# Feed-forward: projecting parts 1 to 8 down in twos, with twelve products to a PSUM bank

## The chip, the cores and the metric

The kernel runs on one core of a Trainium2 chip. The metric is the time of the whole kernel on the device in microseconds; lower is better. A core has five engines that work side by side, each through its own queue in order: TensorE (PE) multiplies matrices into PSUM, VectorE (DVE), ScalarE (ACT) and GpSimd (POOL) work on elements, and SyncE (SP) issues the transfers (DMA) from and to memory.

## The reference, cut to what matters

The program is a two-layer encoder over two sequences, 512 tokens ("sample") and 256 ("prompt"), 768 columns in all, with 1024 channels. Each layer has a mixer and then a feed-forward block, in float32. The change lies in the feed-forward:

```python
def conv_ffn(h, w_up, conv_w, conv_b, w_down):
    u = h @ w_up                      # 1024 -> 2 * 2816 channels
    u = conv(u, conv_w) + conv_b      # width 3 along the tokens, each channel alone
    g = u[..., :D_FF]
    val = u[..., D_FF:]
    return (jax.nn.silu(g) * val) @ w_down   # 2816 -> 1024

x = x + g2 * conv_ffn(h, ...)         # g2: a gate for each channel and sequence
```

## The kernel before, in words

Activations lie transposed in SBUF, channels on the 128 partitions and tokens along the row. Every product of two float32 matrices is made of three products of a high and a low part: weight high by activation high, weight high by activation low, weight low by activation high. The high part is a cast by ScalarE, the low part a subtraction by VectorE (`fp_copy_split`, lines 271 to 279).

The feed-forward of a layer (`ffn`, line 1582 on) cuts the 2816 hidden channels into eleven parts of 256 (`NPART` = 11). A part has three units of weights, each loaded by SP in two halves of 512 KB into one of five `raw` buffers and split into one of three `whi` and three `wlo` buffers (`split`, lines 290 to 293).

`up(p)` makes the hidden values of a part. Two calls of `pair` (gate channels, then value channels) multiply by a scheme of seven quarter products instead of eight; each quarter is twelve products of 384 columns (lines 1360 to 1363). A pair holds three split weight tiles at once (`wa`, `wc`, `wb`); `wc` and `wb` need sums of weight quarters that GpSimd makes from `raw` (lines 1393 to 1405), and between quarters ScalarE copies one bank into another, the fork copies (lines 1409 and 1420). The first part's ups, and a piece of the second's, are made in `head`. After each pair the convolution runs on two rows of channels: one ScalarE instruction and two of VectorE for each row (lines 1597, 1599 and 1600). Then `silu` on ScalarE (1607), and `product`: GpSimd multiplies (1612), and the result is split into its high and low part in a tile `g`.

`down(p, g)` multiplies `g` by the part's third unit: for each of its two weight halves four output tiles of 512 columns and four of 256, six products to a PSUM bank, then one VectorE instruction (the eviction, `resid`, line 604) that multiplies the bank by the gate and adds it to the residual stream `xt`. So a part has 96 down products and 16 evictions. The banks come from `pa`, four of them. The last part works in three ranges of 256 columns and starts the next norm.

The order of the program is up 0, up 1, down 0, up 2, down 1, and so on to up 10, down 9, down 10. Each engine's queue is then ordered by a planner that goes through the program with modelled costs: an instruction that stands later in the program may come earlier on its engine where the earlier one is not ready. So in the trace down products lie among the quarter products of the next part. A call within `issue_after` puts what it holds behind a named instruction on that engine. `held` is a list of work that is put off: `pair` takes one entry and issues it behind its fork copy (line 1420).

Long rows lie in six `slab` buffers. During the ups two hold `xt`, one the rows `urow`, and the rest `yrow` (the convolved rows of a part) and `g`. The tiles `urow` of the first part are a slab of their own, free after its convolution.

Of the kernel before, what the change touches and what calls it, by code (L numbers as in the profile page):

```python
# [12 lines left out]
R = mybir.dt.float32r  # L13
# [3 lines left out]
P = 128  # L17
# [7 lines left out]
RANGES = ((256, 512, 0), (512, 768, 0), PROMPT)  # L25
# [5 lines left out]
TG = T + GAP  # L31
# [3 lines left out]
NPART = FC // 2  # L35
# [45 lines left out]
def col(t):  # L81

    return t + (GAP if t >= 256 else 0)
# [7 lines left out]
class Norm:  # L91
# [31 lines left out]
    held = False  # L123
# [58 lines left out]
class Net:  # L182
# [1399 lines left out]
    def ffn(self, l, xt, pool, last_tile, apply, keep=None):  # L1582
        nc = self.nc
        u0 = U_FFN + l * NPART * 3
        early = self.prepare(u0)
        next(last_tile)

        urows = [self.slab([P, 4, TG]) for _ in range(2)]
        for urow in urows:
            nc.gpsimd.memset(urow[:, :, 256 : 256 + GAP], 0.0)  # L1590

        behind = []

        def conv(u, y, ch):
            cb = self.cst(CB + l * 44 + ch)
            w = lambda tap: self.cst(CW + (l * 44 + ch) * 3 + tap)
            nc.scalar.activation(y, u, AF.Identity, bias=cb, scale=w(1))  # L1597
            stt = nc.vector.scalar_tensor_tensor
            stt(y[:, 1:], u[:, :-1], w(0), y[:, 1:], ALU.mult, ALU.add)  # L1599
            stt(y[:, :-1], u[:, 1:], w(2), y[:, :-1], ALU.mult, ALU.add)  # L1600


        held = []

        def silu(yrow):
            for j in range(2):
                nc.scalar.activation(yrow[:, j], yrow[:, j], AF.Silu)

        def product(yrow, g):
            for j in range(2):  # L1610
                y = yrow[:, 2 + j]
                nc.gpsimd.tensor_tensor(y, y, yrow[:, j], ALU.mult)  # L1612
                self.fp_copy_split(g[:, 0, j], g[:, 1, j], y)

        def up(p):
            urow = urows[0] if p == 0 else urows[1]
            fixed = lambda i: self.bank[i][:, :H]
            if p == 0:
                eng = mybir.EngineType
                self.ready(HALVES[0])  # L1620
                with self.tc.manual_schedule(engines={eng.PE, eng.Activation, eng.DVE}):
                    behind[:] = self.head(u0, last_tile, pool, urows, mark, early)
            yrow = self.slab([P, 4, TG])
            g = self.slab([P, 2, 2, TG], R)
            for i in range(2):
                if p:
                    rows = [urow[:, 2 * i + j] for j in range(2)]
                    with ExitStack() as order:
                        for ins in behind[2 * i :] if p == 1 else ():
                            order.enter_context(self.tc.issue_after(ins))  # L1630

                        other = p == i == 1
                        bank = lambda j: self.pa()[:, :H] if j == 1 and other else fixed(j)
                        self.pair(pool, u0 + 3 * p + i, bank, rows, p == 1, held.pop() if held else None)
                for j in range(2):
                    conv(urow[:, 2 * i + j], yrow[:, 2 * i + j], i * FC + 2 * p + j)
                if i == 0:
                    held.append(lambda: silu(yrow))
            if p:
                product(yrow, g)  # L1640
            else:
                gate = held.pop()
                held.append(lambda: (gate(), product(yrow, g)))
            return g

        def mark(t):

            hi, _ = self.quarter(self.B11)
            self.mm(t, hi[0][:, :P], hi[0], True, True)

        def down(p, g):
            ws = (w for _, w in self.halves(u0 + 3 * p + 2))
            chunk = lambda w, i: [t[:, 512 * i : 512 * (i + 1)] for t in w]

            def tile(w, c, rng, more=False):
                s0, s1, _ = rng
                alone = keep is None and p == NPART - 1
                o = (self.ps() if more and (c % 2 or alone) else self.pa())[:, : s1 - s0]
                cs = slice(c % 4 * P, (c % 4 + 1) * P)
                for i in range(2):  # L1660
                    wh, wl = chunk(w, i)
                    gh, gl = (g[:, z, i, col(s0) : col(s0) + s1 - s0] for z in range(2))
                    self.mm(o, wh[:, cs], gh, i == 0, False)
                    self.mm(o, wh[:, cs], gl, False, False)
                    self.mm(o, wl[:, cs], gh, False, i == 1)
                return self.resid(xt, o, l, 40, c, rng)

            if p < NPART - 1:
                for h, w in enumerate(ws):
                    for rng in SAMPLE, PROMPT:  # L1670
                        for c in range(4 * h, 4 * h + 4):
                            tile(w, c, rng, p == NPART - 2)
                return
            ws = list(ws)
            for rng in RANGES:
                final = keep is None and rng is RANGES[-1]
                norm = Norm(
                    self, xt, rng, apply, 3 if final else 4 if keep is None and rng is RANGES[1] else 2, final,
                    wait=0.0 if keep is None or rng is RANGES[-1] else 1.3,
                )  # L1680
                for c in range(KC):
                    done = tile(ws[c // 4], c, rng, keep is None or rng is not RANGES[-1])
                    norm.square(c)
                    if final and c >= KC - 2:
                        self.ends.append(done.ins)
                    if final and c == KC - 1:
                        norm.sums = [norm.sums[i] for i in (1, 2, 0, 3)]
                        norm.begin(1)
                    self.tick(0.65)
                if keep is not None:  # L1690
                    self.save_x(xt, keep, rng)
                self.start(rng, norm.stages())

        prev = None
        for p in range(NPART):
            g = up(p)
            if prev is not None:
                down(*prev)
            prev = (p, g)
        down(*prev)  # L1700


    def run(self):
# [179 lines left out]
```

## Time and profile before

| | |
|---|---|
| time, median of 3 runs | 1803.56 us (1803.45 to 1805.8) |
| the profiled execution | 1807.31 us, of which its span is 1805.3 us |
| VectorE, share of the span | 77% |
| ScalarE | 50% |
| GpSimd | 28% |
| evictions and gated sums of line 604, 128x512 from `pa` | 152, 743 ns each |
| of 128x256 from `pa` | 168, 476 ns each |

The profile is of one execution. Busy time of PE is modelled from the starts of its products, which overlap, so the distance between starts says more than the length of one. Rows of a timeline give the start, the length, the engine, the line of the kernel, the operation, the tiles written and read, the shape and the count of instructions merged into the row; a bracket at the end gives the engine's idle time before it and who ended that.

### The profile page before, as it was taken

The page shows a single profiled execution, that of the slowest core. Times are in us where ns is not written, and L with a number is a line of the kernel's source. Part 1 is how long each engine was busy: PE and PEld are TensorE (multiplying, and loading weights), DVE is VectorE, ACT ScalarE, POOL GpSimd, SP SyncE. Part 2 cuts the span into 40 slices and gives each one's busy share as a digit, 9 for nine tenths or more (in the row PEclk, how much of TensorE's full clock was granted, in tenths as well). Part 3 has the DMA queues.
Part 4 walks back from the last instruction along what each step waited for, and adds up shares of the span by engine and source line. Part 5 has one row for each costly group of instructions (what it writes and reads, how often), then busy time and mean ns, then how long its engine had stood idle before and what let it go on. Part 6 is the DMA issues. An engine that isn't in the chain of part 4 may idle for free.

```text
span 1805.3 us, 28807 instructions
## 1 busy us (share of the span) xinstructions
PE 1765.0 (98%) x11140; PEld 1641.3 (91%) x11140; DVE 1397.3 (77%) x2196; ACT 900.3 (50%) x1822; POOL 510.1 (28%) x433
## 2 busy tenths in 40 slices
PE   7999999989999999999999999999999999999998
PEld 4988888979998999999999999989989999999997
DVE  4876677996799777788877867767998777777877
ACT  4545443443564444444444657665564444444443
POOL 3001010231134233333331313320234333333323
PEclk9999999999999999999999999999999999999999
DMA  9354665467212222222222321234122222222212
GB/s 359 99 163 148 207 197 188 151 187 233 71 59 71 71 62 68 70 70 71 70 70 84 108 91 42 62 99 128 47 82 70 71 71 70 71 71 71 70 36 71
DMA packets 64996, 185.07 MB, mean 103 GB/s; under 512 B 6247, under 2 KB 24839, under 8 KB 64732
## 3 DMA queue, kind: packets, MB, share of 16 engines
q1 hardware_dynamic: 64284, 182.72, 31.8%
q8 instruction: 87, 1.43, 0.3%
q10 hardware_dynamic: 576, 0.52, 0.1%
q14 instruction: 49, 0.40, 0.1%
HBM read 176.77 MB, written 6.44 MB: 101 GB/s over the span
## 4 chain that ended last, share of the span: by engine, by line
PE 84%; DVE 6%; DMA 5%; ACT 3%; issue 2%; POOL 1%; SPq 0%; DVEq 0%; ACTq 0%; POOLq 0%
PE ps L269 26%; PE pa L269 23%; PE ps L1360 10%; PE ps L1361 10%; PE ps L1363 10%; DMA raw<-in_adaln_t_dram 2%; DVE junk L540 1%; PE pa L1199 1%; DMA raw<-in_w_dram 1%; DMA slab<-in_adaln_w_dram 1%; DVE wlo L276 1%; ACT whi L275 0%; PE pa L1360 0%; PE pa L1361 0%; PE pa L1363 0%
## 5 line engine op out<-in xcount | busy, mean ns | idle before, releaser
L275 ACT CAST whi<-raw 128x1024 fp32r<-128x1024 f32 (+1 forms) x231 | 241.0, 1045 | 339.2 <-PE pa L269 144.0
L276 DVE TENSOR_TENSOR wlo<-raw,whi 128x1024 fp32r<-128x1024 f32 (+1 forms) x231 | 318.5, 1380 | 112.7 <-ACT whi L275 110.0
L269 PE MATMUL pa<-slab,whi 128*128 128x256 f32 (+1 forms) x1280 | 307.6, 335 | 0.0
L269 PEld LDWEIGHTS pa<-slab,whi 128*128 128x128 f32 x1280 | 222.2, 188 | 21.6 <-DVE slab L604 0.4
L604 DVE SCALAR_TENSOR_TENSOR slab<-pa,mod,slab 128x256 f32<-128x256 f32 (+1 forms) x320 | 187.2, 603 | 61.4 <-PE pa L269 61.3
L269 PE MATMUL pa<-slab,wlo 128*128 128x512 f32 (+1 forms) x640 | 205.8, 334 | 0.0
L269 PE MATMUL ps<-zh,whi 128*128 128x256 f32 (+1 forms) x560 | 187.4, 336 | 5.0 <-ACT whi L275 4.8
L269 PE MATMUL ps<-zl,whi 128*128 128x256 f32 (+1 forms) x560 | 183.2, 330 | 0.5 <-DVE zl L565 0.5
L269 PE MATMUL ps<-zh,wlo 128*128 128x256 f32 (+1 forms) x560 | 180.6, 329 | 0.2 <-DVE wlo L276 0.2
L1360 PE MATMUL ps<-zh,whi 128*128 128x384 f32 x504 | 172.6, 343 | 3.8 <-ACT nt L1431 2.0
L269 PE MATMUL ps<-slab,whi 128*128 128x384 f32 (+2 forms) x704 | 172.0, 329 | 0.9 <-DVE slab L276 0.5
L1361 PE MATMUL ps<-zl,whi 128*128 128x384 f32 x504 | 170.0, 337 | 1.8 <-DVE zl L1317 1.8
L540 DVE CUSTOM_DVE_ANT_0 junk<-raw,crow,cstt 128x1024 f32<-128x1024 f32 x112 | 148.6, 1327 | 27.8 <-DMA raw<-in_adaln_t_dram 27.1
L1363 PE MATMUL ps<-zh,wlo 128*128 128x384 f32 x504 | 169.2, 336 | 0.0
L1396 POOL TENSOR_TENSOR raw<-raw,raw 128x512 f32<-128x512 f32 x40 | 53.7, 1342 | 318.5 <-DVE wlo L276 245.8
L1612 POOL TENSOR_TENSOR slab<-slab 128x772 f32<-128x772 f32 x44 | 86.4, 1966 | 168.8 <-DVE slab L1600 155.9
L269 PEld LDWEIGHTS pa<-slab,wlo 128*128 128x128 f32 x640 | 120.4, 188 | 13.2 <-DVE wlo L276 0.4
L1599 DVE SCALAR_TENSOR_TENSOR slab<-slab,cstt,slab 128x771 f32<-128x771 f32 x88 | 107.6, 1224 | 27.1 <-ACT slab L1597 26.9
L269 PEld LDWEIGHTS ps<-slab,whi 128*128 128x128 f32 x704 | 122.4, 188 | 3.4 <-ACT whi L275 0.9
L269 PEld LDWEIGHTS ps<-zh,whi 128*128 128x128 f32 x560 | 106.4, 190 | 18.2 <-ACT whi L275 5.0
L269 PE MATMUL ps<-slab,wlo 128*128 128x384 f32 (+2 forms) x352 | 114.8, 328 | 0.1
L269 PEld LDWEIGHTS ps<-zl,whi 128*128 128x128 f32 x560 | 106.3, 190 | 9.3 <-DVE zl L565 0.7
(304 smaller groups left out, 4297.2 us busy)
## 6 DMA issues: line engine op xcount, KB each, us to landing
raw<-in_w_dram SPq DMA_DIRECT2D x208, 512.0 KB, 3.8
raw<-in_adaln_t_dram SPq DMA_DIRECT2D x56, 512.0 KB, 4.1
raw<-in_adaln_w_dram SPq DMA_DIRECT2D x28, 512.0 KB, 4.4
slab<-in_x_dram SPq DMA_DIRECT2D x12, 512.0 KB, 8.2
slab<-in_adaln_w_dram SPq DMA_DIRECT2D x11, 512.0 KB, 9.2
slab<-mrows SPq DMA_DIRECT2D x8, 384.0 KB, 6.7
xs<-slab SPq DMA_DIRECT2D x6, 512.0 KB, 2.9
bt<-brow SPq DMA_DIRECT2D x16, 192.0 KB, 3.1
```

The lines of the kernel that those rows point to most:

```text
L269: self.nc.tensor.matmul(out, lhsT, rhs, start=start, stop=stop)
L275: nc.scalar.copy(hi, src)
L276: return nc.vector.tensor_tensor(lo, src, hi.bitcast(F32), ALU.subtract)
L540: nc.vector.tensor_tensor_reduce(out=junk, in0=w, in1=row[:, s], scale=1.0, scalar=self.cst(AB + 48 * l + j), op0=ALU.mult, op1=ALU.add, a ...
L604: return self.nc.vector.scalar_tensor_tensor(x, o, self.mod[l][:, gc + c, q : q + 1], x, ALU.mult, ALU.add)
L1199: nc.tensor.transpose(pp[:, ks], b.t[:, e, ks], self.ident)
L1360: mm(o, wh[:, k], hi[k], start=start and k == 0, stop=False, skip_group_check=True)
L1361: mm(o, wh[:, k], lo[k], start=False, stop=False, skip_group_check=True)
L1363: mm(o, wl[:, k], hi[k], start=False, stop=k == 3, skip_group_check=True)
L1396: tt(q[0], q[2], q[0], ALU.subtract)
L1599: stt(y[:, 1:], u[:, :-1], w(0), y[:, 1:], ALU.mult, ALU.add)
L1612: nc.gpsimd.tensor_tensor(y, y, yrow[:, j], ALU.mult)
```

## The change

Parts 1 to 8 go down in twos: after up 3 the parts 1 and 2, after up 5 the parts 3 and 4, after up 7 the parts 5 and 6, after up 9 the parts 7 and 8. Part 0 (after up 1), part 9 and part 10 (both after up 10) go alone as before. In a joined down both parts' products of one output tile go into one bank, twelve instead of six, and are evicted once. Both parts' weight halves are split and held together, first halves, then second halves.

The tile `g` is now made when it is first written, and `yrow` after the part's first pair. For the odd parts 3, 5, 7 and 9 GpSimd's multiplication stays where it was, and the split of its result is put into `held`, so that it comes behind the fork copy in the next part's first pair. The count of products, their columns and the loads are the same.

```diff
+        gs = {}
+
+        def product(yrow, p, now):
+            def part(j):
+                if not j:
+                    gs[p] = self.slab([P, 2, 2, TG], R)
+                self.fp_copy_split(gs[p][:, 0, j], gs[p][:, 1, j], yrow[:, 2 + j])
+
             for j in range(2):
                 y = yrow[:, 2 + j]
                 nc.gpsimd.tensor_tensor(y, y, yrow[:, j], ALU.mult)
-                self.fp_copy_split(g[:, 0, j], g[:, 1, j], y)
+                if now:
+                    part(j)
+            if not now:
+                held.append(lambda: [part(j) for j in range(2)])
...
             if p:
-                product(yrow, g)
+                product(yrow, p, p in (1, NPART - 1) or p % 2 == 0)
...
-        def down(p, g):
-            ws = (w for _, w in self.halves(u0 + 3 * p + 2))
+        def down(parts):
+            of = [self.halves(u0 + 3 * p + 2) for p in parts]
+            g = [gs.pop(p) for p in parts]
...
+                steps = [(w, x, i) for w, x in zip(ws, g) for i in range(2)]
+                for w, x, i in steps:
                     wh, wl = chunk(w, i)
-                    gh, gl = (g[:, z, i, col(s0) : col(s0) + s1 - s0] for z in range(2))
-                    self.mm(o, wh[:, cs], gh, i == 0, False)
+                    gh, gl = (x[:, z, i, col(s0) : col(s0) + s1 - s0] for z in range(2))
+                    self.mm(o, wh[:, cs], gh, w is ws[0] and i == 0, False)
                     self.mm(o, wh[:, cs], gl, False, False)
-                    self.mm(o, wl[:, cs], gh, False, i == 1)
+                    self.mm(o, wl[:, cs], gh, False, w is ws[-1] and i == 1)
                 return self.resid(xt, o, l, 40, c, rng)
...
-            if p < NPART - 1:
-                for h, w in enumerate(ws):
+            if parts[0] < NPART - 1:
+                for h in range(2):
+                    ws = [next(x)[1] for x in of]
                     for rng in SAMPLE, PROMPT:
                         for c in range(4 * h, 4 * h + 4):
-                            tile(w, c, rng, p == NPART - 2)
+                            tile(ws, c, rng, parts[-1] == NPART - 2)
                 return
...
-        prev = None
         for p in range(NPART):
-            g = up(p)
-            if prev is not None:
-                down(*prev)
-            prev = (p, g)
-        down(*prev)
+            up(p)
+            if p % 2:
+                down((p - 2, p - 1) if p > 1 else (0,))
+        down((p - 1,))
+        down((p,))
```

More of the change, by code (lines that the diff above doesn't have):

```diff
@@ L1607, in silu @@
                 nc.scalar.activation(yrow[:, j], yrow[:, j], AF.Silu)
-        def product(yrow, g):
+        gs = {}
[4 more added lines that the diff above has]
+                self.fp_copy_split(gs[p][:, 0, j], gs[p][:, 1, j], yrow[:, 2 + j])
             for j in range(2):
@@ L1622, in up @@
                     behind[:] = self.head(u0, last_tile, pool, urows, mark, early)
-            yrow = self.slab([P, 4, TG])
-            g = self.slab([P, 2, 2, TG], R)
+            yrow = None
             for i in range(2):
@@ L1634, in up @@
                         self.pair(pool, u0 + 3 * p + i, bank, rows, p == 1, held.pop() if held else None)
+                yrow = yrow or self.slab([P, 4, TG])
                 for j in range(2):
@@ L1639, in up @@
             if p:
-                product(yrow, g)
+                product(yrow, p, p in (1, NPART - 1) or p % 2 == 0)
             else:
                 gate = held.pop()
-                held.append(lambda: (gate(), product(yrow, g)))
-            return g
+                held.append(lambda: (gate(), product(yrow, p, True)))
         def mark(t):
@@ L1649, in mark, with tile @@
             self.mm(t, hi[0][:, :P], hi[0], True, True)
-        def down(p, g):
-            ws = (w for _, w in self.halves(u0 + 3 * p + 2))
+        def down(parts):
+            of = [self.halves(u0 + 3 * p + 2) for p in parts]
+            g = [gs.pop(p) for p in parts]
             chunk = lambda w, i: [t[:, 512 * i : 512 * (i + 1)] for t in w]
-            def tile(w, c, rng, more=False):
+            def tile(ws, c, rng, more=False):
                 s0, s1, _ = rng
-                alone = keep is None and p == NPART - 1
+                alone = keep is None and parts[0] == NPART - 1
                 o = (self.ps() if more and (c % 2 or alone) else self.pa())[:, : s1 - s0]
                 cs = slice(c % 4 * P, (c % 4 + 1) * P)
-                for i in range(2):
+                steps = [(w, x, i) for w, x in zip(ws, g) for i in range(2)]
+                for w, x, i in steps:
                     wh, wl = chunk(w, i)
-                    gh, gl = (g[:, z, i, col(s0) : col(s0) + s1 - s0] for z in range(2))
-                    self.mm(o, wh[:, cs], gh, i == 0, False)
+                    gh, gl = (x[:, z, i, col(s0) : col(s0) + s1 - s0] for z in range(2))
+                    self.mm(o, wh[:, cs], gh, w is ws[0] and i == 0, False)
                     self.mm(o, wh[:, cs], gl, False, False)
-                    self.mm(o, wl[:, cs], gh, False, i == 1)
+                    self.mm(o, wl[:, cs], gh, False, w is ws[-1] and i == 1)
                 return self.resid(xt, o, l, 40, c, rng)
-            if p < NPART - 1:
-                for h, w in enumerate(ws):
+            if parts[0] < NPART - 1:
+                for h in range(2):
+                    ws = [next(x)[1] for x in of]
                     for rng in SAMPLE, PROMPT:
                         for c in range(4 * h, 4 * h + 4):
-                            tile(w, c, rng, p == NPART - 2)
+                            tile(ws, c, rng, parts[-1] == NPART - 2)
                 return
-            ws = list(ws)
+            ws = [w for _, w in of[0]]
             for rng in RANGES:
@@ L1681, in down @@
                 for c in range(KC):
-                    done = tile(ws[c // 4], c, rng, keep is None or rng is not RANGES[-1])
+                    done = tile(ws[c // 4 : c // 4 + 1], c, rng, keep is None or rng is not RANGES[-1])
                     norm.square(c)
```

## The prediction

> **What bounds the kernel now.** I read the head of the page first.
>
> ```profile
> span 1805.3 us, 28807 instructions
> PE 1765.0 (98%) x11140; PEld 1641.3 (91%) x11140; DVE 1397.3 (77%) x2196; ACT 900.3 (50%) x1822; POOL 510.1 (28%) x433
> ```
>
> TensorE is busy nearly always, but a mean over stages proves nothing for the feed-forward, so I read a window over one of its parts, from the last product of one part's ups to that of the next. The columns are length, then busy time and instructions of PE, PE's weight loads, VectorE (DVE), ScalarE (ACT) and GpSimd (POOL), the granted clock, and the DMA engines' share and GB/s.
>
> ```profile
> 740.02:786.40 46.38, 46.38 (x266) 43.98 (x265) 37.49 (x42) 21.61 (x35) 16.69 (x10) 1.00 0.22 69
> ```
>
> One part is 46.4 us, all of it PE, at a granted clock of 1.00; DVE is busy 37 us of it. Since a busy PE could hide slow starts, the timeline must give the pace. These rows are a quarter product's first product and the next quarter's first, twelve on; then down products of 512 columns, two to a row; then of 256 columns, two and one.
>
> ```profile
> 773.59 0.34 PE L1360 MATMUL ps<-zh,whi 128*128 128x384 f32 x1
> ...
> 775.68 0.34 PE L1360 MATMUL ps<-zh,s1h 128*128 128x384 f32 x1
> ...
> 744.98 0.62 PE L269 MATMUL pa<-slab,whi 128*128 128x512 f32 x2
> 745.44 0.62 PE L269 MATMUL pa<-slab,wlo 128*128 128x512 f32 x2
> ...
> 763.09 0.40 PE L269 MATMUL pa<-slab,whi 128*128 128x256 f32 x2
> 763.33 0.28 PE L269 MATMUL pa<-slab,wlo 128*128 128x256 f32 x1
> 763.45 0.39 PE L269 MATMUL pa<-slab,whi 128*128 128x256 f32 x2
> ```
>
> Starts are 2.09/12 = 0.174 us apart at 384 columns, 0.46/2 = 0.23 at 512 and 0.36/3 = 0.12 at 256. A part has 14 quarter products (29.26 us) and 96 down products (48 x 0.23 + 48 x 0.12 = 16.8 us): 46.06 us of work in a 46.38 us period, so 0.32 us per part is all that is not products. Last I asked what PE waits for in the stretch from part 2's ups to the last part, and who waits for the evictions (L604).
>
> ```profile
> engine line waited for: us in total, times, longest us
> PE ps L1360 <- ACT ps L1420: 0.2, 1, 0.2
> ```
>
> ```profile
> L604 DVE SCALAR_TENSOR_TENSOR slab<-pa,mod,slab x112: 466/610/753, 652.2 to 951.3; 128x512 f32<-128x512 f32 x56, 128x256 f32<-128x256 f32 x56
> its engine sat idle before it (us, times) until:
>   PE pa L269: 26.4, 42
> who waited for it (us, times):
> ```
>
> From 553 to 975 us PE has one listed wait, 0.2 us, for ScalarE's fork copy. In 650 to 960 us, 112 evictions waited 26.4 us for PE, and nobody waited for one.
>
> **The change part by part.** *Evictions removed.* For each two parts one set of 8 + 8 goes. The rows of five parts, 693.66 to 925.56 us, with each group's count, busy time and mean:
>
> ```profile
> L276 DVE TENSOR_TENSOR wlo<-raw,whi 128x1024 fp32r<-128x1024 f32 x41 | 60.3, 1471 | 22.6 <-ACT whi L275 22.2
> L604 DVE SCALAR_TENSOR_TENSOR slab<-pa,mod,slab 128x512 f32<-128x512 f32 x40 | 29.3, 744 | 7.6 <-PE pa L269 7.6
> L1599 DVE SCALAR_TENSOR_TENSOR slab<-slab,cstt,slab 128x771 f32<-128x771 f32 x20 | 26.7, 1333 | 7.6 <-ACT slab L1597 7.5
> L1600 DVE SCALAR_TENSOR_TENSOR slab<-slab,cstt,slab 128x771 f32<-128x771 f32 x20 | 25.0, 1252 | 0.2
> L604 DVE SCALAR_TENSOR_TENSOR slab<-pa,mod,slab 128x256 f32<-128x256 f32 x40 | 18.3, 477 | 10.9 <-PE pa L269 10.9
> L276 DVE TENSOR_TENSOR slab<-slab,slab 128x772 fp32r<-128x772 f32 x10 | 11.8, 1176 | 0.0
> L276 DVE TENSOR_TENSOR s1l<-raw,s1h 128x512 fp32r<-128x512 f32 x10 | 10.5, 1055 | 0.1
> L1434 DVE TENSOR_TENSOR slab<-ps,nt 128x384 f32<-128x384 f32 x11 | 6.0, 547 | 0.0
> L1433 DVE TENSOR_TENSOR slab<-ps,nt 128x384 f32<-128x384 f32 x10 | 5.5, 551 | 2.0 <-PE ps L1363 2.0
> ```
>
> 8 x 0.744 + 8 x 0.477 = 9.77 us, times 4 twos, times 2 layers: 78 us less DVE work. None of it is on the path: the count of products and their columns is unchanged, PE does not wait for these evictions, and 26.4 us of DVE's idleness there is waiting for PE. Worth 0. If all of the 0.32 us per part went, the 16 joined parts would give 5.1 us; but the one wait listed there is for a ScalarE copy, which stays.
>
> *The order.* Now up, down, up, down becomes up, up, both downs. Nothing stands between the even up and the odd one, four times a layer. I call that place the seam. It puts more DVE work per PE time into the pair behind it: PE has 7 x 2.09 = 14.63 us; DVE has the even part's last convolutions (2 x 1.333 + 2 x 1.252 = 5.17), its product's two splits (2.35), three weight splits (4.41), s1's (1.06) and two sums (1.10): 14.09 us, 96%. Within a part, without the product, it is 11.7 us, 80%. The trace has one place with two ups in a row, part 0 to part 1, before the first down:
>
> ```profile
> 526.33:557.61 31.28, 28.08 (x152) 26.44 (x153) 31.24 (x30) 21.60 (x34) 13.82 (x7) 1.00 0.33 101
> 536.00:552.23 16.23, 13.16 (x72) 12.17 (x71) 16.19 (x13) 11.64 (x19) 10.37 (x5) 1.00 0.31 97
> 740.02:761.16 21.14, 21.14 (x116) 19.05 (x114) 19.96 (x24) 8.48 (x12) 8.88 (x5) 1.00 0.20 59
> ```
>
> There DVE is full for 31 us and PE loses 16.23 - 13.16 = 3.07 us: the upper bound of a seam. The third row is the lower: DVE 94% busy for 21 us behind a part's end, PE lost nothing, though down products filled the gaps in it. Part 1's stretch carries all eight convolutions of part 0 beside its own first ones, against ten quarter products; the seam has four against seven, so it is nearer to the third row. I take 0.3 us, a tenth of the upper bound: 8 x 0.3 = 2.4 us. Bounds 0 to 24.6 us. Below nothing is excluded, since PE has no wait there to lose.
>
> The even product's splits also free the slab that the odd part's first convolution writes. In the trace its last split begins at
>
> ```profile
> 756.52 0.96 DVE L276 TENSOR_TENSOR slab<-slab,slab 128x772 fp32r<-128x772 f32 x1
> ```
>
> and ends 17.5 us after the pair's end at 740.02; the convolution would want it after 14.63. In between stand eight evictions, 4 x 0.744 + 4 x 0.477 = 4.9 us, that are no longer there: about 12.6 us, so 0; uncovered, 2.9 us on ScalarE's queue, ahead of its weight casts.
>
> *Two weight halves at a time.* The buffers for split weights are three. A joined down keeps two for a half of 48 x 0.23 + 48 x 0.12 = 16.8 us. At its middle the second part's next half needs the buffer that the first part's half frees 6 x 0.12 = 0.72 us before the last tile ends, and PE has 6 x 0.23 = 1.38 us more of the other half: 2.1 us. To fill it takes
>
> ```profile
> L275 ACT CAST whi<-raw 128x1024 fp32r<-128x1024 f32 x41 | 43.0, 1049 | 74.3 <-PE pa L269 41.6 <-POOL raw L1397 15.9 <-PE ps L1361 14.7
> ```
>
> 1.05 + 1.47 = 2.52 us, but the low half is first read by the third product, 0.46 later. That is level. Behind one convolution it would be 1.3 us late; three other banks' first halves (3 x 1.38) can run meanwhile if the planner orders them so. I take 0, bounds 0 to 8 x 1.3 = 10.4 us. The four loads per two parts are the same, only in another order on SP:
>
> ```profile
> raw<-in_w_dram SPq DMA_DIRECT2D x208, 512.0 KB, 3.8
> ```
>
> 3.8 us each against 92.8 us for two parts' twelve, with DMA at 0.22: nothing.
>
> *The later split.* An odd part's two casts and two DVE splits (2.35 us) go behind a fork copy in the next pair, on ScalarE ahead of that pair's later copies. Their slab is freed by the joined down, which is ahead of that fork; their reader is two ups away, 58.5 us. Cost 0; if the slab were late, those copies wait and PE with them. SP and POOL have nothing moved past them, but POOL's work now falls into the ups: 2 x 16.7 us in 58.5 us, 57%. Not a bound.
>
> *Sum.* +2.4 us on the profiled execution, 1807.31 us (span 1805.3 and 2.0 around it): 1809.7. That execution is 3.75 us above the median of the three runs, 1803.56; on the median it is **1806.0 us**. About 0.2% (3.6 us) is what a measurement of this kernel can tell from no change, so this counts as the same.
>
> **Where the skill speaks.** A convolution behind a part's end took 1.02 us, another 2.14 us when a POOL instruction began beside it:
>
> ```profile
> 742.30 1.02 DVE L1599 SCALAR_TENSOR_TENSOR slab<-slab,cstt,slab 128x771 f32<-128x771 f32 x1
> ...
> 771.64 2.14 DVE L1599 SCALAR_TENSOR_TENSOR slab<-slab,cstt,slab 128x771 f32<-128x771 f32 x1 [1.16 <-ACT slab L1597]
> ...
> 771.67 1.29 POOL L1393 TENSOR_TENSOR raw<-raw 128x512 f32<-128x512 f32 x1 [0.80 <-DMA raw<-in_w_dram]
> ```
>
> The Trainium skill's page "SBUF — State Buffer", section "Who interferes with whom", says that a VectorE instruction with two SBUF inputs contends with a GpSimd one that reads SBUF, and that one with at most one SBUF input does not. By that rule the change removes only the kind that never contends (an eviction reads one input from PSUM; the 112 above stay within 466 to 753 ns over both sizes) and crowds the kind that does. That speaks against the change, and the first rival has its size.
>
> **The rivals.**
>
> *The seam is DVE's (slower).* Both multiplications of the even product now fall into one pair of 14.63 us instead of into 46 us:
>
> ```profile
> L1612 POOL TENSOR_TENSOR slab<-slab 128x772 f32<-128x772 f32 x10 | 18.6, 1861 | 31.9 <-DVE slab L1600 31.9
> ```
>
> If one of them, 1.86 us, holds DVE up beyond the means above, the pair has 15.95 us of DVE work: 1.3 us over, 8 times, 10.6 us: 1814.2 us. It decides from where DVE's work passes 14.63 us. For it: the 3.07 us at part 1. Against it: a pair's weights may be split ahead, and the second pair of the odd part is at 80%. Chance 0.27.
>
> *The halves come late (slower).* 1.3 us at each of the eight middles: 1814.0 us. For it: three buffers, two held. Against it: other banks' products to run. Chance 0.12.
>
> *The rest of the period goes (faster).* An easier DVE lets ScalarE's copies start earlier and the 0.32 us per part vanish: 1803.56 - 5.1 = 1798.4 us. Against it: the listed wait is on a copy whose own input is PE's. Chance 0.07.
>
> *The pace itself rises (faster).* If the 0.23 and 0.12 us of the down products were stretched by evictions, halving those would return part of it; against it, quarter products keep 0.174 us in 773.59 to 775.68, where no eviction runs, so the stretch is not theirs. If products ran a twentieth slower beneath an eviction (assumed, no row shows it), the 78 us of evictions that go would give 3.9 us: 1799.7 us. Chance 0.02. The Trainium skill's page "TensorE: Matmul & The Clock Gate", section "Back-to-back issue gap", gives N/2.4 + 2.5 ns, or 216 ns at 512 columns and 109 ns at 256; by an estimate from that page the pace has about 7% to give, and the trace differs from it in all three widths.
>
> **How the numbers follow.** The forecast, no change that can be told, has 0.52. Slower by over 0.2%: 0.27 + 0.12 = 0.39. Faster: 0.07 + 0.02 = 0.09. The range is 1801.5 to 1815.0 us: upwards it takes in both slower rivals at their price and leaves out a seam near 3.07 us (about 0.08); downwards it leaves out the faster ones (0.09).
>
> **What would show it.** Right: 64 fewer L604 rows of 512 columns and 64 fewer of 256; DVE about 78 us less busy; two parts still in 92.7 to 93.1 us; no PE wait over 0.5 us between parts 2 and 9. Wrong: PE waits for wlo, s1l or whi in an odd part's pairs (the first rival) or at a joined down's middle (the second); or two parts in under 92.4 us.

## The result, and the profile after

| | before | after |
|---|---|---|
| time, median (lowest to highest), 19 runs each | 1804.58 us (1803.16 to 1807.21) | 1807.89 us (1806.08 to 1810.13) |
| ratio, 95% interval | | 1.0019 [1.0011, 1.0026] |

The change costs 3.4 us, between 2.0 and 4.7. That is just within the 0.2% (3.6 us) that the prediction counted as no change, and its interval excludes zero. The forecast of 1806.0 us was 2.4 us above its base of 1803.56.

The head of the page after:

```profile
span 1806.2 us, 28731 instructions
PE 1765.5 (98%) x11140; PEld 1643.0 (91%) x11140; DVE 1306.8 (72%) x2068; ACT 899.3 (50%) x1822; POOL 508.3 (28%) x433
```

VectorE has 2196 - 2068 = 128 instructions less, and is busy 90.5 us less. TensorE does the same products in the same busy time. The lines of 693.66 to 925.56 us, which the prediction read for the kernel before (count, busy time, mean of one, then the idle time before the group):

```profile
L276 DVE TENSOR_TENSOR wlo<-raw,whi 128x1024 fp32r<-128x1024 f32 x40 | 59.5, 1497 | 15.1 <-ACT whi L275 14.9
L1600 DVE SCALAR_TENSOR_TENSOR slab<-slab,cstt,slab 128x771 f32<-128x771 f32 x22 | 22.3, 1012 | 0.2
L1619 POOL TENSOR_TENSOR slab<-slab 128x772 f32<-128x772 f32 x12 | 27.1, 2257 | 41.4 <-DVE slab L1600 32.2 <-ACT whi L275 9.2
L604 DVE SCALAR_TENSOR_TENSOR slab<-pa,mod,slab 128x512 f32<-128x512 f32 x20 | 14.9, 746 | 17.1 <-PE pa L269 17.1
L276 DVE TENSOR_TENSOR slab<-slab,slab 128x772 fp32r<-128x772 f32 x10 | 9.4, 953 | 4.4 <-ACT slab L275 4.4
L604 DVE SCALAR_TENSOR_TENSOR slab<-pa,mod,slab 128x256 f32<-128x256 f32 x18 | 8.7, 484 | 16.3 <-PE pa L269 16.3
```

The evictions are halved, and one still takes 746 or 484 ns. The second convolution step and the product's split became quicker, GpSimd's multiplication slower (line 1619, before 1612: 2257 ns, was 1861). Line numbers up to 1605 are as before.

What TensorE waits for in the feed-forward of layer 1 (553 to 985 us), with total, times and longest:

```profile
engine line waited for: us in total, times, longest us
PE ps L1360 <- ACT ps L1409: 1.7, 4, 0.4
PE pa L269 <- DVE slab L604: 0.9, 1, 0.9
```

Layer 2 has the same: 1.7, 4, 0.4 and 0.8, 1, 0.8. Before, each layer had one wait of 0.2 us here. The four waits for the fork copy of line 1409 come once in every two parts, in the odd part. The windows of parts 4 and 5 show where. Columns as in the prediction. The rows are the even part's second pair, the odd part's first pair (the seam lies between them, at 697.74), and the beginning of the odd part's second pair; then two whole parts; then the stretch of the joined down.

```profile
683.10:697.74 14.64, 14.64 (x85) 14.64 (x85) 10.14 (x12) 9.63 (x17) 3.82 (x3) 1.00 0.23 73
697.74:712.38 14.64, 14.64 (x85) 14.64 (x85) 12.30 (x12) 9.64 (x16) 9.82 (x5) 1.00 0.23 72
712.38:726.26 13.88, 13.46 (x73) 12.64 (x73) 9.77 (x10) 9.58 (x16) 2.41 (x2) 1.00 0.36 115
634.00:726.70 92.70, 92.28 (x530) 87.73 (x529) 60.93 (x65) 42.95 (x68) 32.75 (x20) 1.00 0.22 69
630.81:668.98 38.17, 38.17 (x221) 33.94 (x220) 22.02 (x28) 8.89 (x12) 11.06 (x7) 1.00 0.16 52
```

In the pair behind the seam (697.74 to 712.38) VectorE is busy 12.30 of 14.64 us, 84%, and TensorE loses nothing. It loses 13.88 - 13.46 = 0.42 us in the stretch after it, where VectorE has time to spare. So the wait is not for a full VectorE. The chain of waits, followed back from the wait, names the way (start, length, engine, tile and line):

```profile
704.07 1.06 ACT whi L275
705.15 2.58 DVE wlo L276
707.80 1.97 POOL raw L1396
709.83 1.29 POOL raw L1397
711.12 1.98 POOL raw L1405
713.12 1.05 ACT whi L275
714.18 0.43 ACT slab L1373 x2
714.61 0.39 ACT ps L1409
715.05 0.45 PE ps L1360
```

Read it from below. TensorE waits for the fork copy (L1409). The copy stands on ScalarE behind two short copies (L1373) and a weight cast. That cast waits for the last of GpSimd's three sums, and these could begin only when VectorE had made the low half of `wa`, which took 2.58 us. GpSimd's own rows say why:

```profile
698.83 2.86 POOL L1619 TENSOR_TENSOR slab<-slab 128x772 f32<-128x772 f32 x1 [3.06 <-ACT whi L275]
704.19 2.45 POOL L1619 TENSOR_TENSOR slab<-slab 128x772 f32<-128x772 f32 x1 [2.50 <-DVE slab L1600]
707.80 1.96 POOL L1396 TENSOR_TENSOR raw<-raw,raw 128x512 f32<-128x512 f32 x1 [1.16 <-DVE wlo L276]
```

The second multiplication of the even part's product runs from 704.19 to 706.64, and the low split lies on top of it. By the starts of TensorE's products the wait is 0.56 to 0.60 us, and the next product is 0.10 us late too: 0.69 us, eight times, 5.5 us. At up 2, beside the down of part 0, stands a further wait in each layer, of about 1.1 us, for an eviction (L604). All stalls over 0.025 us in the two feed-forwards add to 3.8 us before and 7.8 us after. The same products, counted from the feed-forward's start, end 1.0 us later in layer 1 and 1.6 us in layer 2: 2.6 us, so 1.4 us of the 4.0 comes back in spacings too small to list.

### The profile page after: what moved, and what is told of

It is laid out like the page before. It is cut to its first block, busy times and chain, and to the rows that moved or that the text cites. A ratio compares the mean times of both kernels' runs of the same rounds, so it can differ in the third digit from the quotient of the medians.

```text
span 1806.2 us, 28731 instructions
## 1 busy us (share of the span) xinstructions
PE 1765.5 (98%) x11140; PEld 1643.0 (91%) x11140; DVE 1306.8 (72%) x2068; ACT 899.3 (50%) x1822; POOL 508.3 (28%) x433
## 4 chain that ended last, share of the span: by engine, by line
PE 76%; DVE 7%; DMA 5%; ACT 4%; POOL 4%; issue 3%; SPq 0%; POOLq 0%; DVEq 0%; ACTq 0%
PE ps L269 26%; PE pa L269 22%; PE ps L1360 9%; PE ps L1361 8%; PE ps L1363 8%; DVE wlo L276 2%; DMA raw<-in_adaln_t_dram 2%; ACT whi L275 2%; PE pa L1199 1%; DVE junk L540 1%; DMA raw<-in_w_dram 1%; POOL raw L1396 1%; POOL raw L1405 1%; DMA slab<-in_adaln_w_dram 1%; POOL raw L1397 1%
## 5 line engine op out<-in xcount | busy, mean ns | idle before, releaser
L276 DVE TENSOR_TENSOR wlo<-raw,whi 128x1024 fp32r<-128x1024 f32 (+1 forms) x231 | 324.6, 1412 | 81.3 <-ACT whi L275 79.6
L269 PEld LDWEIGHTS pa<-slab,whi 128*128 128x128 f32 x1280 | 217.6, 188 | 26.8 <-DVE slab L604 2.7
L269 PE MATMUL pa<-slab,wlo 128*128 128x256 f32 (+1 forms) x640 | 207.0, 334 | 0.0
L604 DVE SCALAR_TENSOR_TENSOR slab<-pa,mod,slab 128x512 f32<-128x512 f32 (+1 forms) x192 | 113.8, 601 | 124.8 <-PE pa L269 124.7
L1619 POOL TENSOR_TENSOR slab<-slab 128x772 f32<-128x772 f32 x44 | 99.3, 2257 | 178.0 <-DVE slab L1600 141.7
L1599 DVE SCALAR_TENSOR_TENSOR slab<-slab,cstt,slab 128x771 f32<-128x771 f32 x88 | 114.7, 1305 | 36.0 <-ACT slab L1597 35.7
L1396 POOL TENSOR_TENSOR raw<-raw,raw 128x512 f32<-128x512 f32 x40 | 60.7, 1517 | 252.6 <-DVE wlo L276 206.1
L1393 POOL TENSOR_TENSOR raw<-raw 128x512 f32<-128x512 f32 x40 | 70.0, 1750 | 210.0 <-DMA raw<-in_w_dram 158.3
L1597 ACT ACTIVATE slab<-slab,cstt 128x772 f32<-128x772 f32 x88 | 91.2, 1036 | 59.7 <-DVE slab L1433 57.7
```

What stands on the lines that cost most here:

```text
L269: self.nc.tensor.matmul(out, lhsT, rhs, start=start, stop=stop)
L276: return nc.vector.tensor_tensor(lo, src, hi.bitcast(F32), ALU.subtract)
L604: return self.nc.vector.scalar_tensor_tensor(x, o, self.mod[l][:, gc + c, q : q + 1], x, ALU.mult, ALU.add)
L1396: tt(q[0], q[2], q[0], ALU.subtract)
```

## The experiments

The first theory was the chain just read: the multiplication on GpSimd lengthens a split, and ScalarE's queue hands that on. Its rivals were that the order itself costs it, that the evictions' saving was never worth anything, and that ScalarE's queue alone is at fault. Times are medians beside runs of the kernel before on the same chip.

### The order without joining

```diff
-                down((p - 2, p - 1) if p > 1 else (0,))
+                for x in (p - 2, p - 1) if p > 1 else (0,):
+                    down((x,))
```

> The changed order alone: both ups, then both downs, but each part projected alone, six products to a bank, 16 evictions a part as before. Seam theory (the loss of the change is in the odd part's second pair, where the even part's product runs on GpSimd and VectorE with no down products to fill): the eight PE waits of 0.58 us stay, 3 us slower than before, ratio 1.0010 to 1.0025. Joining theory (the loss comes from two weight halves held at a time or from the longer banks): the loss goes, ratio 1.0000 within 0.0005.

Measured: 1822.13 against 1805.22 us, ratio 1.0097 [1.0081, 1.0112]. Its waits in layer 1's feed-forward, read as above:

```profile
engine line waited for: us in total, times, longest us
PE pa L269 <- DVE slab L604: 3.5, 5, 0.8
PE ps L1360 <- ACT ps L1409: 1.8, 4, 0.5
PE ps L1360 <- ACT ps L1420: 0.6, 3, 0.2
```

The order alone costs 17.5 us, and joining the downs gives 17.5 - 3.4 = 14.1 us back. By the starts of the same products the order makes layer 1's feed-forward 8.3 us longer and layer 2's 9.0. Neither expectation had a loss of this size. Now TensorE does wait for evictions, which nobody did in the kernel before: by the starts, waits for an eviction cost 8.0 us more in the two feed-forwards than in the joined kernel, and shorter stalls the other 6 us or so.

### The evictions without the order

The kernel before, where parts 1, 3, 5 and 7 are multiplied but not added, so their 16 evictions each are left out.

```diff
+                if p in (1, 3, 5, 7):
+                    return None
                 return self.resid(xt, o, l, 40, c, rng)
```

> The kernel before, in its order, without the evictions of parts 1, 3, 5 and 7 (their down products are made and not added). Forecast's step (evictions are worth nothing): ratio 1.0000 within 0.0005, VectorE some 70 to 90 us less busy. If relief of VectorE is worth something: 2 to 5 us faster, ratio 0.9972 to 0.9990.

Measured: 1803.68 us, ratio 0.9991 [0.9983, 1.0000]: a gain of 1.6 us, at most twice that and perhaps none. So in the old order the evictions are worth next to nothing. In the new order joining, which takes away as many, is worth 14 us, 8.0 of them in waits for an eviction. What an eviction costs depends on the order that it stands in.

### One multiplication left out

The second multiplication of parts 2, 4, 6 and 8 is left out of the changed kernel.

```diff
-                nc.gpsimd.tensor_tensor(y, y, yrow[:, j], ALU.mult)
+                if not (j and p in (2, 4, 6, 8)):
+                    nc.gpsimd.tensor_tensor(y, y, yrow[:, j], ALU.mult)
```

> The changed kernel without GpSimd's second multiplication in parts 2, 4, 6 and 8 (their second channel block is projected unmultiplied by the gate). Chain theory: wa's low split behind the seam falls from 2.58 to 1.2 us, GpSimd's three sums come over 2 us earlier, the eight waits of 0.58 us go, ratio to before 0.9990 to 1.0000. Work theory: VectorE's own instructions are all there, the waits stay at over half, ratio 1.0010 to 1.0019.

Measured: 1802.42 us, ratio 0.9986 [0.9977, 0.9995], 6 us less than the change. The four waits are gone:

```profile
engine line waited for: us in total, times, longest us
PE pa L269 <- DVE slab L604: 1.1, 1, 1.1
```

VectorE's timeline at the same place as the chain above:

```profile
703.94 2.00 DVE L276 TENSOR_TENSOR slab<-slab,slab 128x772 fp32r<-128x772 f32 x2
705.92 1.23 DVE L276 TENSOR_TENSOR wlo<-raw,whi 128x1024 fp32r<-128x1024 f32 x1
```

The low split takes 1.23 us where it took 2.57. The multiplication beside it is what stretched it. The same holds throughout the changed kernel: 166 of these splits have no GpSimd multiplication or sum beside them and take 1.22 us in the mean, 75 have one and take 1.86. The Trainium skill's page "SBUF — State Buffer", section "Who interferes with whom", says that VectorE and GpSimd contend when the one reads two inputs from SBUF and the other reads SBUF. The trace agrees: the split of two SBUF inputs doubles, and the eviction with one input in PSUM kept its 746 ns.

The split is only a part of what reaches TensorE. GpSimd's three sums, without that multiplication:

```profile
707.23 1.29 POOL L1396 TENSOR_TENSOR raw<-raw,raw 128x512 f32<-128x512 f32 x1 [5.57 <-DVE wlo L276]
708.60 1.29 POOL L1397 TENSOR_TENSOR raw<-raw 128x512 f32<-128x512 f32 x1
709.84 1.30 POOL L1405 TENSOR_TENSOR raw<-raw,raw 128x512 f32<-128x512 f32 x1
```

The split ends 0.6 us earlier than in the change, and so the sums begin 0.6 us earlier. The sums themselves take 3.9 us where they took 5.3. In the change the first and the last of them had begun just behind a VectorE instruction with two SBUF inputs, the product's second split (707.64) and a convolution step (710.69). The last sum ends at 711.14 where it ended at 713.09, 1.95 us earlier, and the other seven places show the same.

### ScalarE's queue

The fork copy comes ahead of the cast in the program, first by order alone, then with the cast held behind it.

```diff
-        wb = self.split(rb)
...
         nc.scalar.copy(b, fork)
+        wb = self.split(rb)
```

> The changed kernel with the fork copy issued ahead of the split of wb in each pair. Chain theory (the late link is ScalarE's queue: the fork copy stands behind the cast of wb, which waits for GpSimd's sum): the eight waits of 0.58 us go, 4 to 5 us less than the change, ratio to before 0.9990 to 1.0000. Work theory (VectorE has too much to do in the seam, whatever the order): the wait only moves to wc's split, ratio 1.0019 as the change.

Measured: 1808.05 us, ratio 1.0017 [1.0009, 1.0026], with the same four waits (1.7 us). The planner put the cast ahead of the copy again, so this run tells nothing of the queue.

```diff
-        wb = self.split(rb)
...
-        nc.scalar.copy(b, fork)
+        first = nc.scalar.copy(b, fork)
+        with self.tc.issue_after(first.ins):
+            wb = self.split(rb)
```

> The changed kernel with wb's cast held behind the fork copy on ScalarE's queue by force. In the second run of experiments the planner had put the cast ahead of the copy again, so the queue was not yet tried. Chain theory with ScalarE's queue as its last link: the eight waits of 0.58 us go, 4 to 5.5 us less than the change, ratio to before 0.9987 to 0.9998. If the late sums themselves are the last link (wc's or wb's split is late whatever ScalarE does first): the wait only moves to another row, ratio 1.0010 to 1.0020.

Measured: 1805.86 against 1804.99 us, ratio 1.0000 [0.9991, 1.0008]. All that is left in layer 1's feed-forward:

```profile
engine line waited for: us in total, times, longest us
PE pa L269 <- DVE slab L604: 0.7, 1, 0.7
```

ScalarE's order is the last link, then. The multiplications still run on GpSimd, and the last sum ends as late as in the change: some 1.4 us ahead of the moment at which TensorE could take the product behind the fork copy, in both kernels. With the order changed that lateness no longer reaches TensorE. By the ratios it gives 3.4 us of the 5.5. Some is lost in the first parts, ahead of this stretch, where the same forced order makes other waits: those of layer 1 from 430 to 553 us sum to 4.3 us, were 3.9. By the starts the first parts are 0.4 us longer in layer 1 and 2.6 us in layer 2, where 1.1 us of such a difference also stands between other kernels, with no edit there.

### The multiplication on VectorE

All products of the changed kernel are multiplied by VectorE:

```diff
-                nc.gpsimd.tensor_tensor(y, y, yrow[:, j], ALU.mult)
+                nc.vector.tensor_tensor(y, y, yrow[:, j], ALU.mult)
```

> The changed kernel with every product's multiplication on VectorE, none on GpSimd: 44 instructions of some 1.0 to 1.3 us more for VectorE, about 50 us of the 90 that the change freed. Contention theory (GpSimd's multiplication holds up VectorE's low split and its own sums): the waits of 0.58 us go, also the one of 1.0 us at part 0's down, ratio to before 0.9975 to 0.9995. Work theory (VectorE has too much to do in the seam): slower than the change, ratio over 1.0025.

Measured: 1796.87 against 1804.99 us, ratio 0.9946 [0.9933, 0.9959]. It beats both kernels. TensorE has no listed wait in either feed-forward. The head of its page, and the same lines as above:

```profile
span 1791.3 us, 28694 instructions
PE 1762.3 (98%) x11140; PEld 1644.7 (92%) x11140; DVE 1305.9 (73%) x2112; ACT 899.9 (50%) x1822; POOL 405.7 (23%) x389
```

```profile
L276 DVE TENSOR_TENSOR wlo<-raw,whi 128x1024 fp32r<-128x1024 f32 x40 | 49.4, 1245 | 12.0 <-ACT whi L275 11.5
L1619 DVE TENSOR_TENSOR slab<-slab 128x772 f32<-128x772 f32 x12 | 11.5, 959 | 0.2
L276 DVE TENSOR_TENSOR s1l<-raw,s1h 128x512 fp32r<-128x512 f32 x10 | 6.9, 688 | 7.2 <-ACT s1h L275 7.2
```

VectorE does 44 instructions more, 42 us of work, and is busy 1305.9 us where it was 1306.8: its other instructions are shorter by as much, the low split of the weights by 252 ns in the mean, now that fewer GpSimd instructions run beside them. By the starts of the same products, this kernel gains on the change 4.2 and 3.9 us in the two feed-forwards and 2.2 and 2.5 us in the first parts before them: 12.7 us of the 13 by the ratios (1.0019 - 0.9946).

Only the even parts from 2 on:

```diff
-                nc.gpsimd.tensor_tensor(y, y, yrow[:, j], ALU.mult)
+                mult = nc.vector if p and p % 2 == 0 else nc.gpsimd
+                mult.tensor_tensor(y, y, yrow[:, j], ALU.mult)
```

> The changed kernel with the multiplications of parts 2, 4, 6, 8 and 10 alone on VectorE. Contention theory: the waits of 0.58 us go, those at part 0's down stay, ratio to before 0.9985 to 1.0000. Work theory: 2 x 1.2 us more in the seam's pair, the waits grow, ratio over 1.0025.

Measured: 1803.02 us, ratio 0.9989 [0.9980, 0.9998]. That is 5.4 us less than the change, and the four waits per layer are gone, one eviction's wait of 0.8 us being left. It is the size of the seam's waits, 5.5 us, without leaving out any work.

All products on VectorE together with the forced order of the fork copy, by the two diffs above:

> The changed kernel with every multiplication on VectorE and wb's cast held behind the fork copy. Chain theory: with the multiplications gone from GpSimd there is no PE wait left at the fork copies between parts 2 and 9, so the forced order has nothing to gain there: ratio 0.9946 within 0.0012. If the lead-in's wait of 1.1 us at the fork copy can go too: up to 2 us less, ratio 0.9930 to 0.9940.

Measured: 1796.35 us, ratio 0.9955 [0.9942, 0.9969], not to be told from the kernel without it. Where the sums are in time, the queue behind them costs nothing.

### The later split undone

```diff
                 down((p - 2, p - 1) if p > 1 else (0,))
+                if held:
+                    held.pop()()
```

> The changed kernel with the odd parts' splits (3, 5, 7, 9) issued right after the joined down, not behind the fork copy of the next pair. The forecast held the later split to cost nothing and hide nothing: ratio 1.0019 within 0.0007. If the place behind the fork copy keeps ScalarE's queue free for the next pair's casts: slower by another 1 to 5 us, ratio over 1.0025.

Measured: 1810.30 us, ratio 1.0028 [1.0018, 1.0037], with the waits of the change (1.6, 4, 0.4 and 0.8, 1, 0.8). The intervals overlap. By the starts the two feed-forwards are 1.9 us longer, with a stall of 0.2 us at a fork copy (L1409) once more in every two parts, too short for the list. The later split is worth between nothing and some 3 us by the times, and about 2 us by the trace.

### VectorE's multiplication without the joined downs

The same edit in the kernel before, and in the kernel with the order alone.

```diff
-                nc.gpsimd.tensor_tensor(y, y, yrow[:, j], ALU.mult)
+                nc.vector.tensor_tensor(y, y, yrow[:, j], ALU.mult)
```

The kernel before with it:

> The kernel before, in its own order and with its own evictions, with every product's multiplication on VectorE. If the gain of the same edit on the changed kernel needs the VectorE time that the joined downs freed: no gain here, ratio 0.9980 to 1.0010, with PE waits behind evictions in the stretch between a part's end and the next pair. If the gain is only that GpSimd no longer holds VectorE up: as much here as there, ratio 0.9940 to 0.9965.

Measured: 1815.60 against 1804.48 us, ratio 1.0060 [1.0047, 1.0072]. It is slower by 11 us, which no theory had said. Its waits in layer 1's feed-forward:

```profile
engine line waited for: us in total, times, longest us
PE ps L1360 <- ACT ps L1420: 4.9, 7, 0.7
```

The timeline at one of the seven:

```profile
670.39 1.05 ACT L275 CAST whi<-raw 128x1024 fp32r<-128x1024 f32 x1 [5.97 <-PE pa L269]
670.91 2.35 DVE L276 TENSOR_TENSOR wlo<-raw,whi 128x1024 fp32r<-128x1024 f32 x2
671.34 0.47 ACT L1420 COPY ps<-ps 128x384 f32<-128x384 f32 x1
671.87 0.19 PEld L1360 LDWEIGHTS ps<-zh,whi 128*128 128x128 f32 x1 [1.01 <-ACT ps L1420]
```

ScalarE sat idle 5.97 us before a cast whose buffer TensorE's last down product frees, and the fork copy stood behind that cast. It is the same kind of link as the seam's, a copy behind a waiting cast, at another fork. By the starts of the products the seven cost 0.96 us each, 13.5 us in both layers. The kernel before has the same pair of instructions there and lost 0.2 us; why the last down product comes later relative to the fork here, no run tells. The seven are not the whole account. Of the two profiled executions, which are 8 us apart, this one's feed-forwards are 10.3 us longer behind their first parts (less than 13.5, since small stalls of the kernel before are gone), its first parts are 6.3 us shorter, and 4.9 us of the loss lie in layer 2's mixer.

The order alone with it:

> The changed order with each part projected alone, six products to a bank, and every product's multiplication on VectorE. The order alone cost 17 us, of which the odd parts' second pairs were 5 and the waits for evictions and other copies the rest. If the longer banks' worth lies in the evictions that PE waits for in two downs in a row: these stay, ratio 1.0000 to 1.0060. If all of those 17 us came of GpSimd's multiplications: ratio 0.9940 to 0.9965, as with the joined downs.

Measured: 1807.81 us, ratio 1.0018 [1.0009, 1.0027]; its waits in layer 1's feed-forward:

```profile
engine line waited for: us in total, times, longest us
PE pa L269 <- ACT whi L275: 1.0, 1, 1.0
PE pa L269 <- DVE slab L604: 0.9, 1, 0.9
PE ps L1360 <- ACT ps L1420: 0.6, 3, 0.2
```

In the order alone VectorE's multiplication saves 14 us (1.0097 to 1.0018), and takes away four of the five waits for an eviction, although the downs are not joined here either. Joining is worth 13 us by the ratios (1.0018 to 0.9946). By the starts of the same products 5.8 and 2.9 us of that lie in the feed-forwards. Another 3.6 us lie in layer 2's mixer, where this kernel and the one before it have one wait of 2.2 us for `zl` (L565) that the others lack; no edit touches that place, and what brings it is open.

## Why the prediction was right, and where it was not

*The sum.* +2.4 us was forecast, +3.4 measured, and the two feed-forwards of the profiles show +2.6. The number held, in part by luck. In the trace the eight seams cost 5.5 us, the waits at up 2 another 2.2, which stood in no term, and against them 3.8 us of small stalls went, which the sum had put at nothing.

*Evictions, worth 0.* Their size was read well: 78 us from the counts, 90.5 measured, the rest being other VectorE instructions that became shorter. In the old order the worth is at most small (1.6 us, down to none), as said. The step that fails is to carry that zero into the new order: there joining is worth 14.1 us, 8.0 of it in waits for an eviction. "Nobody waited for one" is true of the order in which it was read.

*The order, 0.3 us a seam.* This term was too small. Taken after the evictions, as the prediction did, it is 1.0019 - 0.9991, or 5 us; the waits say 0.69 us each, 5.5 us. Taken first, it is 17.5 us, inside the bounds of 0 to 24.6, which the trace's one place with two ups in a row had set. What made the sum right is that most of the order's cost and of the joining's gain fall on the same waits and cancel.

*The place.* The prediction watched VectorE in the first pair behind the seam and forecast 96%. It was 84%, and TensorE lost nothing there: a weight split and a convolution step of those counted had run just ahead of it, and others were shorter, the product's splits 0.95 us each where 1.18 was taken. The 0.69 us came in the second pair, which the prediction had set aside at 80%. A share of busy time could not find it. A chain could have: `wb` needs the sum that needs `wa`'s low half, and the fork copy stands behind the cast of `wb`.

*The first rival (0.27).* Its cause was the true one. The even product's multiplication on GpSimd holds a VectorE split up by 1.34 us (2.57 against 1.23). That this is almost the 1.3 us of its price is chance, for the price came from a full VectorE: here VectorE is far from full, against the condition given. What is late is handed on through GpSimd's sums, the last of which ends 1.95 us late, and through ScalarE's queue, where slack leaves 0.69. Its sign, a wait for `wlo`, `s1l` or `whi` in an odd part, did not come: the row names the fork copy. Against that stand the 0.2 us stalls of each part before, which went. So the time came out at the forecast, with the rival's mechanism at half its price. Skipping that multiplication, or moving it, takes the waits away; that is shown. The Trainium skill's rule in "SBUF — State Buffer", section "Who interferes with whom", weighed in the prediction, pointed at it.

*Two halves at a time, 0.* Right. The joined down of 630.81 to 668.98 us is 38.17 us with TensorE busy for all of it, middle included. The second rival is out.

*The slab of `yrow`, the loads, the later split.* The first two are right as far as seen: no wait names them. The later split, put at nothing, makes nothing slower, and is worth perhaps 2 us.

*The rest of the period.* The third rival was wrong for this change as a whole, though the 0.2 us stalls of each part did go. It was not wrong as to what there was to win: with the multiplications on VectorE all listed waits of the feed-forward are gone, and by the starts the two feed-forwards behind their first parts are 4.7 us shorter than before, where the rival had 5.1. The fourth, a pace that rises, has nothing for it: products of 512 and of 256 columns start 0.232 and 0.118 us apart in the feed-forwards of both kernels.

*The signs named.* The 128 evictions and two parts in 92.70 us came as said. "No wait over 0.5 us between parts 2 and 9" failed: at the seams by a little (the list gives 0.4 us, the starts of the products 0.58), and at up 2, with 0.9 us for an eviction, by more.

## What to carry to other kernels

When a change reorders work and also removes some, price the removal in the new order, not in the trace of the old one: here the order cost 17.5 us, the joining that removes evictions gave 14.1 back, and each read alone in the old trace looked like almost nothing. Look for a short copy that TensorE needs behind a cast that waits for something else on the same queue; the chain of waits shows it, and shares of busy time don't. Try to give VectorE the elementwise work with SBUF inputs that GpSimd does beside it, and measure it in each order: the same edit gained 13 us in the changed kernel and 14 in the order alone, and cost 11 in the kernel before, 4.9 of them at a place that stays open. When it pays isn't shown.

## What the runs showed of the hardware

Multiplying two rows of 128x772 took GpSimd 1.86 us on average before and 2.26 us after, and VectorE 0.96 us. Moving 44 of them to VectorE left VectorE's busy time as it was, 1306.8 to 1305.9 us, so what they cost VectorE itself, 42.2 us, came back from its other instructions: 29 us from the low splits of the weights and some 11 from the other splits and the convolutions. Without a GpSimd instruction beside it a low split takes 1.22 us in the changed kernel, with one 1.86 in the mean; a GpSimd sum of 128x512 takes 1.29 us, and 1.96 to 2.01 where a VectorE instruction with two SBUF inputs had begun just before it (at 707.80 and 711.08 in the change). The evictions of 512 columns, with one input in PSUM, were 744 to 749 ns in the mean in the kernel before, the change and the one with all multiplications on VectorE.
